# Four of nine weight-sum DMAs issued in the gate phase, and g2 spread over the partitions by two fp32r products

## The chip, the core and the metric

The kernel runs on one core of one Trainium2 chip. A core has a matrix engine (TensorE, PE in the profile), a vector engine (VectorE, DVE), a scalar engine (ScalarE, ACT), a general engine (GpSimd, POOL), an engine that here only issues transfers (SyncE, SP), and 16 DMA engines. SP and POOL both issue DMAs; in the profile SP's are on queue q1 (hardware_dynamic) and POOL's on queue q0 (software_dynamic). The metric is the time of one execution on the device, in microseconds.

## The reference

One layer of a diffusion backbone with a pooling mixer and a SwiGLU channel mixer, all in fp32. x is 1024 tokens by 1024 features, and F = 2816.

```
mod = silu(c) @ mod_w + mod_b            # 1024 x 6144, split in sh1, sc1, g1, sh2, sc2, g2
hx  = x * (1 + sc1) + sh1
ox  = pool_scale * (windowed means of hx, minus hx, per group, @ pool_w)
x   = layer_norm(ALPHA * x + g1 * ox)
h   = x * (1 + sc2) + sh2
gt, up = split(h @ w_in)                 # w_in 1024 x 5632
x   = layer_norm(ALPHA * x + g2 * ((silu(gt) * up) @ w_out))     # w_out 2816 x 1024
```

## The kernel before

**Precision.** Each fp32 operand of a large product is split into an fp32r part (take_hi, a cast on ACT, line 267) and the fp32r rest (take_lo, a subtraction on DVE, line 270). Three fp32r products on PE (high by high, high by low, low by high) then stand for one fp32 product.

**Stages.** From 0 to 92 us of the profile's span the modulation sums, the pooling and the first layer norm of the first 512 tokens are computed. From 92 to 237 the gate phase runs: 11 pairs of 128-wide column blocks of w_in, each with 8 `gate_step`s on PE (line 761), for the first half of the tokens, mixed with the pooling and the layer norm of the second half. From 237 to 551 the first product of the FFN runs in 22 periods, one for each column block of w_in. It is done by a scheme like Strassen's: it takes seven products of 512-wide halves of tokens and features, and sums of blocks, instead of eight products. From 551 to 778 the second product of the FFN (line 1088) runs in seven passes, with the last layer norm.

**Gate phase.** A table of names, `ORDER_OF_ISSUE`, sets the order in which the pieces of this phase are written, and thereby each engine's order. `gate_load` brings 512 KB of w_in (rows of 1 KB) into a tile wi, `gate_hi` and `gate_lo` split it, `gate_step` multiplies. A pair has two loads, one for each half of the features, and two halves of four steps. After the first half, `gate_first` copies the partial sums from PE's banks into the tile pk on ACT (line 766); after the second, `gate_done` applies silu into gk (line 771); `gate_out` writes pk and gk to memory (pd and gd), from where the FFN's periods read them again. ACT takes its casts in the order in which they are written, and so does DVE its subtractions.

**FFN periods.** Period f issues on SP four loads of 256 KB of w_in for period f + 2 (`weights_load`, tile raw), one load of pd or gd, and in periods 5 to 12 a load of mod_w for g2. POOL sums the loaded weights (`all_sums`, four operations); ACT and DVE split the results (w0h, w0l, ws and so on); PE multiplies (`first_product`, line 895). DVE and ACT form the activations in tiles a, whose blocks and sums are stored by SP (a11d, a2d, s21d, s43d), and the stored tiles free the places of the next ones. Big tiles share 45 places, taken in order.

**Weight sums.** The second product needs four sums of blocks of w_out, e1 to e4, each 1408 by 512 (2816 KB). They are built in memory by nine DMAs, `e_step(0)` to `e_step(8)`, issued from POOL (line 1039). Steps 0 and 1 write a block plainly, steps 2, 3, 6, 7 and 8 add a block to what is there (`accum_op`), steps 4 and 5 copy one sum to another. In the kernel before, step n is issued in period 1 + 2n (`E_AT`, `E_EVERY`), behind that period's `all_sums` on POOL. A step that writes the same sum as an earlier one waits for it: 2 for 0, 3 for 1, 4 for 2, 5 for 3, and so on.

**g2.** The modulation row g2 is summed over features as 128 partial rows in the tile acc (`mod_add`, line 491, in periods 6 to 13). In periods 14 and 15 `g2_half` adds the 128 rows and spreads the sum over all partitions: a product of a matrix of ones with acc, in fp32 on PE (line 870), once for each 512 columns. DVE copies each result to g2.

Of the kernel before, what the change touches and what calls it, by code (L numbers as in the profile page):

```python
# [13 lines left out]
F32R = mybir.dt.float32r  # L14
ACT = mybir.ActivationFunctionType
ALU = mybir.AluOpType

P = 128
# [3 lines left out]
KT = D // P  # L22
# [50 lines left out]
gate_step.9 mod_load.34 gate_step.10 mod_load.35 gate_step.11 gate_load.6 gate_load.7 mod_add.29 gate_step.12  # L73
gate_done.0 gate_out.2 gate_step.13 mod_add.30 gate_step.14 mod_add.31 gate_step.15 load_pool_w.2 load_pool_w.3
mod_add.32 gate_hi.6 gate_step.16 mod_load.37 gate_lo.6 gate_first.2 gate_step.17 mod_load.38 gate_out.3 gate_hi.7
gate_step.18 mod_load.39 gate_lo.7 gate_step.19 gate_load.8 gate_load.9 gate_step.20 gate_done.1 gate_out.4
gate_step.21 gate_step.22 mod_add.33 gate_step.23 mod_add.34 gate_first.3 gate_step.24 gate_out.5 gate_step.25
mod_add.35 gate_step.26 gate_hi.8 gate_step.27 gate_load.10 gate_load.11 gate_lo.8 pool_outer.11 gate_done.2
gate_step.28 gate_out.6 gate_hi.9 gate_step.29 gate_lo.9 gate_step.30 gate_step.31 gate_hi.10 gate_lo.10 gate_first.4
gate_step.32 gate_out.7 gate_hi.11 gate_step.33 gate_lo.11 gate_step.34 gate_step.35 gate_load.12 gate_load.13  # L80
gate_step.36 gate_done.3 gate_out.8 gate_step.37 gate_hi.12 gate_step.38 gate_lo.12 gate_hi.13 gate_step.39
gate_first.5 gate_lo.13 gate_step.40 gate_out.9 gate_step.41 gate_step.42 gate_step.43 gate_load.14 gate_load.15
gate_step.44 gate_done.4 gate_out.10 gate_hi.14 gate_step.45 gate_lo.14 gate_step.46 gate_hi.15 gate_step.47
weights_load.0 gate_lo.15 gate_first.6 gate_step.48 gate_out.11 gate_step.49 gate_step.50 gate_step.51 gate_load.16
gate_load.17 all_sums.0 gate_step.52 gate_done.5 gate_out.12 mod_col.3 one_hi.0 one_lo.0 gate_hi.16 gate_step.53
mod_col_done.1 shift_through.0 two_hi.0 pool_inner.56 gate_lo.16 pool_inner.48 gate_hi.17 pool_inner.39 pool_outer.9
pool_inner.57 pool_inner.49 pool_inner.59 gate_lo.17 pool_outer.14 pool_inner.51 pool_outer.12 gate_step.54
shift_through.1 pool_inner.46 pool_inner.38 pool_inner.58 pool_hi.11 pool_inner.50 gate_step.55 two_lo.0 pool_hi.9
gate_first.7 pool_lo.11 gate_step.56 pool_lo.9 gate_out.13 pool_hi.14 pool_inner.60 pool_lo.14 pool_inner.52
pool_hi.12 pool_inner.61 pool_lo.12 pool_inner.53 pool_inner.63 pool_outer.15 pool_inner.55 pool_outer.13  # L90
pool_inner.62 pool_inner.54 pool_hi.15 shift_bank.0 pool_lo.15 pool_hi.13 shift_bank.1 pool_lo.13 gate_step.57
shift_row.0 shift_row.1 gate_step.58 pooled.12 pooled.14 residual.12 bend.0 gate_step.59 gate_load.18 gate_load.19
gate_hi.18 gate_hi.19 residual.14 bend.2 pooled.13 gate_done.6 gate_lo.18 gate_out.14 pooled.15 residual.13 bend.1
pooled.8 residual.15 pooled.10 bend.3 residual.8 gate_step.60 residual.10 gate_lo.19 pooled.9 mean.6 pooled.11
residual.9 spread.6 mean.7 mean.4 gate_step.61 residual.11 spread.7 factor.6 mean.5 gate_step.62 factor.7 spread.4
gate_step.63 p1_load.0 weights_load.1 factor.4 gate_first.8 gate_step.64 gate_out.15 spread.5 gate_step.65 factor.5
norm.6 gate_step.66 keep_row.6 norm.7 gate_step.67 gate_load.20 gate_load.21 norm.4 keep_row.7 norm.5 gate_step.68
keep_row.4 keep_row.5 gate_done.7 gate_step.69 gate_out.16 gate_step.70 gate_hi.20 gate_step.71 gate_lo.20
gate_first.9 gate_step.72 gate_out.17 gate_hi.21 gate_step.73 gate_lo.21 gate_step.74 turned.8 turned.10 scaled_h.8
gate_step.75 scaled_h.10 gate_done.8 turned.12 turned.14 gate_out.18 scaled_h.12 turned.9 scaled_h.14 turned.11  # L100
turned.13 scaled_h.9 turned.15 scaled_h.11 difference.0 gate_step.76 scaled_h.13 scaled_h.15 difference.4 gate_step.77
hidden_hi.4 difference.1 gate_step.78 hidden_hi.5 difference.5 t_hi.0 gate_step.79 gate_first.10 t_lo.0 gate_step.80
gate_out.19 t_hi.4 hidden_lo.4 gate_step.81 difference.2 t_hi.1 gate_step.82 t_hi.5 difference.3 t_hi.2 gate_step.83
t_lo.4 gate_done.9 gate_step.84 t_lo.1 gate_out.20 t_hi.3 gate_step.85 t_lo.5 t_lo.2 gate_step.86 t_lo.3 gate_step.87
gate_done.10 hidden_lo.5 gate_out.21 difference.6 difference.7 t_hi.6 t_lo.6 t_hi.7 t_lo.7
""".split()

ENGINE_OF = {}
# [111 lines left out]
def trunk_kernel(ctx: ExitStack, tc: tile.TileContext, x, c, mod_w, mod_b, ln_g, ln_b, ffn_w_in, ffn_w_out,  # L220
                 pool_w, pool_scale, consts, out):
    nc = tc.nc
    keep = ctx.enter_context(tc.tile_pool(name="keep", bufs=1))
# [34 lines left out]
    def small(name, shape, bufs=1, tag=None):  # L258
        return keep.tile(list(shape), F32, tag=tag or name, name=name, bufs=bufs)
# [12 lines left out]
    def split(hi, lo, src):  # L272
        take_hi(hi, src)
        take_lo(lo, src, hi)
# [16 lines left out]
    tiles = {}  # L291
# [228 lines left out]
    def column_half(h):  # L520
        return slice(h * HALF, (h + 1) * HALF)
# [213 lines left out]
    e_of = [dram.tile([P, NF // 2, HALF], F32, tag=f"e{n}", name=f"ed{n}", bufs=1) for n in range(1, 5)]  # L735
    p1_of, gate_of = spill("p"), spill("g")

    def act_tile(name):
        return take("big", name, F32, (P, 2, HALF))

# [121 lines left out]
    for j in range(2):  # L862
        for n in (1, 3, 2, 4):
            job(difference, n, j)
            job(t_hi, n, j)
            job(t_lo, n, j)

    def g2_half(h):
        ps = bank(f"ps_g2_{h}")
        nc.tensor.matmul(ps, ones, tiles["acc", G2][:, column_half(h)], start=True, stop=True)  # L870
        nc.vector.tensor_copy(g2[:, column_half(h)], ps)
        done_with("bank", f"ps_g2_{h}")

# [148 lines left out]

    first, second = column_half(0), column_half(1)
    whole = slice(0, D)
    w_out = ffn_w_out.rearrange("(j r p) d -> p r j d", p=P, r=2)
    res, lines, raw, operands = {}, {}, {}, {}

    def block(r, h):

        return w_out[:, r, :, column_half(h)]  # L1030


    E_STEPS = [(0, block(0, 1), False), (2, block(0, 1), False), (0, block(0, 0), True), (2, block(1, 1), True),
               (1, 0, False), (3, 2, False), (3, block(0, 0), True), (1, block(1, 1), True), (3, block(1, 0), True)]

    def e_step(n):
        dst, src, add = E_STEPS[n]
        src = e_of[src] if isinstance(src, int) else src
        nc.gpsimd.dma_start(e_of[dst], src, **({"accum_op": ALU.add} if add else {}))


    PARTS = ((lambda j: a11_of[j][:, 0], lambda j: w_out[:, 0, j, first]),
# [133 lines left out]

    E_AT, E_EVERY = 1, 2

    def other_loads(f):
        if f + 2 < NF:
# [62 lines left out]
    with tc.manual_schedule():  # L1245
# [8 lines left out]
        f = NF  # L1254
# [112 lines left out]
```

## Time and profile before

| what | value |
|---|---|
| time, median of 3 runs | 779.75 us (776.33 to 781.9) |
| time of the profiled execution | 779.76 us |
| its span | 778.0 us |
| mean granted clock of PE | 0.954 |
| PE busy | 732.1 us, 94% of the span |
| DVE busy | 571.5 us, 73% |
| ACT busy | 270.5 us, 35% |
| POOL busy | 166.5 us, 21% |
| queue q1 (SP) | 164.97 MB, 61.8% of the 16 engines' span |
| queue q0 (POOL) | 25.95 MB, 15.0% |

Busy times are shares of the span on that engine. PE's clock is what the throttle granted; 1.00 is full speed, and at 0.50 a product takes twice as long. The share of a DMA queue is the time its packets took, divided by that of 16 engines; a share a little over 1 means that all of them are full. Issue rows of SP and POOL begin when the engine issues the transfer; the data move later.

### The profile page before, as it was taken

To read this page: it belongs to the slowest core of one execution; us is meant where nothing else is said; L and a number is where in the kernel's file an instruction comes from. 1 tells how busy PE (TensorE), PEld (TensorE's weight loads), DVE (VectorE), ACT (ScalarE), POOL (GpSimd) and SP (SyncE) were. 2 spreads that over 40 slices of the span, in tenths; PEclk is the share of its full clock that TensorE was granted. 3 is DMA by queue.
4 is the path that set the end of the run, shared out by engine and by line. 5 is a ranking of instruction groups with operands and counts; after the bars stand their busy time and mean duration, and the time that the engine had idled before them with its cause. 6 is when DMAs were issued, how large, how long until landed. Compare 5 with 4: busy or idle time off the path is not lost.

```text
span 778.0 us, 9216 instructions
## 1 busy us (share of the span) xinstructions
PE 732.1 (94%) x3391; PEld 609.7 (78%) x3391; DVE 571.5 (73%) x684; ACT 270.5 (35%) x342; POOL 166.5 (21%) x114
## 2 busy tenths in 40 slices
PE   6939999999999999999999999989999999999991
PEld 6729788888888888887887788768888888888881
DVE  3687734346268888896999796866879659659997
ACT  0324844442983221221221221221557333334201
POOL 0000000020202937164366164260000000000015
PEclk7559999999999999999999999989999999999996
DMA  8999278644636979999999999966899767564202
GB/s 299 351 400 330 109 262 306 230 149 141 228 128 211 339 246 255 288 251 315 330 337 285 262 223 298 208 202 253 284 391 388 274 217 244 187 218 163 109 27 108
DMA packets 117091, 191.51 MB, mean 246 GB/s; under 512 B 7371, under 2 KB 66451, under 8 KB 116918
## 3 DMA queue, kind: packets, MB, share of 16 engines
q1 hardware_dynamic: 108326, 164.97, 61.8%
q0 software_dynamic: 8720, 25.95, 15.0%
q8 instruction: 26, 0.43, 0.2%
q14 instruction: 19, 0.16, 0.1%
HBM read 150.79 MB, written 66.06 MB: 279 GB/s over the span
## 4 chain that ended last, share of the span: by engine, by line
PE 60%; DVE 25%; DMA 7%; issue 3%; ACT 2%; SPq 1%; POOL 0%; POOLq 0%; DVEq 0%; ACTq 0%
PE ps_v L895 17%; PE ps_gate L761 16%; PE ps_x L1088 15%; DMA a11d<-a 4%; PE ps_y L1088 4%; DVE w1l L270 3%; DVE w0l L270 3%; DVE acc L491 2%; DVE ws L270 2%; PE ps_pt L461 2%; DVE ylo L270 2%; DVE yrow L1148 1%; PE ps_ox L263 1%; DVE su L1127 1%; PE ps_ox L264 1%
## 5 line engine op out<-in xcount | busy, mean ns | idle before, releaser
L958 POOL TENSOR_TENSOR s<-raw,raw 128x512 f32<-128x512 f32 x22 | 35.6, 1616 | 353.3 <-DMA raw<-in_ffn_w_in 323.8
L895 PE MATMUL ps_v<-t,w0h 128*128 128x512 f32 x352 | 111.0, 397 | 0.0
L761 PE MATMUL ps_gate<-h,wih 128*128 128x512 f32 x352 | 109.8, 393 | 0.8 <-ACT h L699 0.8
L267 ACT CAST yhi<-yraw 128x1024 fp32r<-128x1024 f32 x77 | 79.3, 1052 | 84.6 <-PE ps_x L1088 32.2
L270 DVE TENSOR_TENSOR ylo<-yraw,yhi 128x1024 fp32r<-128x1024 f32 x77 | 91.5, 1219 | 13.3 <-ACT yhi L267 7.3
L1088 PE MATMUL ps_x<-ylo,yhi 128*128 128x512 f32 (+1 forms) x231 | 87.6, 379 | 0.0
L1088 PE MATMUL ps_x<-yhi 128*128 128x512 f32 (+1 forms) x231 | 87.6, 379 | 0.0
L1088 PE MATMUL ps_x<-yhi,ylo 128*128 128x512 f32 (+1 forms) x231 | 87.5, 379 | 0.0
L918 ACT ACTIVATE a<-a 128x512 f32<-128x512 f32 x22 | 13.9, 632 | 187.7 <-DVE a L917 178.1
L895 PEld LDWEIGHTS ps_v<-t,w0h 128*128 128x128 f32 x352 | 67.2, 191 | 15.0 <-issue 1.0
L761 PEld LDWEIGHTS ps_gate<-h,wih 128*128 128x128 f32 x352 | 65.2, 188 | 14.5 <-ACT h L699 1.0
L491 DVE SCALAR_TENSOR_TENSOR acc<-mw,s_col,acc 128x1024 f32<-128x1024 f32 x40 | 55.3, 1384 | 23.1 <-DMA mw<-in_mod_w 22.9
L895 PE MATMUL ps_v<-t,ws 128*128 128x512 f32 x264 | 66.9, 401 | 4.8 <-DVE ws L270 4.7
L895 PE MATMUL ps_v<-t,w0l 128*128 128x512 f32 x176 | 69.2, 393 | 0.5 <-DVE w0l L270 0.5
L761 PE MATMUL ps_gate<-h,wil 128*128 128x512 f32 x176 | 68.6, 390 | 0.0
L895 PEld LDWEIGHTS ps_v<-t,ws 128*128 128x128 f32 x264 | 50.5, 193 | 17.3 <-DVE ws L270 6.9
L1110 POOL TENSOR_TENSOR yrow<-yrow,line_lg 128x512 f32<-128x512 f32 (+2 forms) x4 | 5.8, 1462 | 239.6 <-ACT yrow L1144 239.6
L895 PE MATMUL ps_v<-h,w1h 128*128 128x512 f32 x176 | 54.2, 389 | 0.0
L895 PE MATMUL ps_v<-t,w1h 128*128 128x512 f32 x176 | 54.2, 389 | 0.0
L1088 PEld LDWEIGHTS ps_x<-ylo,yhi 128*128 128x128 f32 x231 | 43.4, 188 | 8.3
L1088 PEld LDWEIGHTS ps_x<-yhi 128*128 128x128 f32 x231 | 43.4, 188 | 8.2
L1088 PEld LDWEIGHTS ps_x<-yhi,ylo 128*128 128x128 f32 x231 | 43.4, 188 | 8.1
(151 smaller groups left out, 1392.7 us busy)
## 6 DMA issues: line engine op xcount, KB each, us to landing
mw<-in_mod_w SPq DMA_DIRECT2D x48, 512.0 KB, 9.2
raw<-in_ffn_w_in SPq DMA_DIRECT2D x88, 256.0 KB, 7.1
ed<-in_ffn_w_out POOLq DMA_DIRECT2D x7, 2816.0 KB, 22.1
wi<-in_ffn_w_in SPq DMA_DIRECT2D x22, 512.0 KB, 6.8
yraw<-ed SPq DMA_DIRECT2D x44, 256.0 KB, 4.4
yraw<-in_ffn_w_out SPq DMA_DIRECT2D x33, 256.0 KB, 5.5
pd<-pk SPq DMA_DIRECT2D x11, 512.0 KB, 4.9
gd<-gk SPq DMA_DIRECT2D x11, 512.0 KB, 3.1
```

Of the source, the lines that this page charges most:

```text
L263: nc.tensor.matmul(ps, lh, rl, start=False, stop=False)
L264: nc.tensor.matmul(ps, ll, rh, start=False, stop=last)
L267: nc.scalar.copy(hi, src)
L270: nc.vector.tensor_tensor(lo, src, hi.bitcast(F32), ALU.subtract)
L461: nc.tensor.matmul(pt_bank[half, ct][:, a:b], xr[ORDER[half][n]][:, ct * P : (ct + 1) * P], operand, start=n == 0, stop=False, skip_group_ ...
L491: nc.vector.scalar_tensor_tensor(acc, w, s_col[:, k : k + 1], acc, ALU.mult, ALU.add)
L761: nc.tensor.matmul(ps, x, y, start=k == n == 0, stop=k % 4 == 3 and n == 2, skip_group_check=k > 3)
L895: nc.tensor.matmul(ps, x, y, start=fresh and first, stop=last, skip_group_check=not fresh)
L918: nc.scalar.activation(a[:, 1], a[:, 1], ACT.Silu)
L958: nc.gpsimd.tensor_tensor(s, up1, up2, ALU.add)
L1088: nc.tensor.matmul(ps, s[x][:, r * P : (r + 1) * P], t[y][:, d], start=fresh and j == m == 0, stop=j == PAIRS - 1 and m == 2, skip_group_c ...
L1127: nc.vector.bn_stats(st_of[i][:, n, :], res[i][:, s])
```

## The change

Two edits.

1. The first four weight-sum DMAs are issued in the gate phase. A new piece, `e_paced(n, pair)`, stands in the table of the order right behind `gate_first` of pairs 0, 3, 6 and 9. It makes POOL copy one column of that pair's pk tile into a small tile, for which it has to wait until ACT has written pk, and then issues `e_step(n)`. The other five steps are issued in periods 2, 6, 10, 14 and 18 (`E_AT` 2, `E_EVERY` 4). The functions `block` and `e_step` are moved up in the file, without other change.
2. `g2_split` splits acc in period 13, behind its last `mod_add`, by a cast on ACT and a subtraction on DVE. `g2_half` then multiplies the two parts with a matrix of ones in fp32r (`ones_r`, a copy made by ACT at the start).

On POOL, the first rows after the start of the program: before, sums of weights (L958 to L961) stand behind the clearing of acc, and the first weight-sum DMA, ed, follows after three sets of sums.

```order
L382 MEMSET acc_158 128x1024
L958 TENSOR_TENSOR s_1237<-raw_0_1197,raw_1_1200 128x512
L959 TENSOR_TENSOR raw_0_1197<-raw_0_1197 128x512
L960 TENSOR_TENSOR raw_0_1197<-s_1237,raw_0_1197 128x512
L961 TENSOR_TENSOR raw_1_1200<-raw_1_1200,raw_0_1197 128x512
...
L1039 DMA ed_120<-in_ffn_w_out 1408x1x512
L958 TENSOR_TENSOR s_2062<-raw_0_1957,raw_1_1960 128x512
```

In the same place of the changed kernel:

```order
L386 MEMSET acc_161 128x1024
L758 COPY pace<-pk_816 128x1
L754 DMA ed_121<-in_ffn_w_out 1408x1x512
L758 COPY pace<-pk_984 128x1
L754 DMA ed_123<-in_ffn_w_out 1408x1x512
L758 COPY pace<-pk_1212 128x1
L754 DMA ed_121<-in_ffn_w_out 1408x1x512
L990 TENSOR_TENSOR s_1246<-raw_0_1204,raw_1_1207 128x512
...
L758 COPY pace<-pk_1672 128x1
L754 DMA ed_123<-in_ffn_w_out 1408x1x512
```

Three of the early DMAs now stand ahead of the first weight sums, and the fourth behind two sets of them; each has a copy of a pk tile ahead of it, which waits for ACT.

On DVE, at the end of the sums for g2 in period 13, the changed kernel has one more row, the subtraction, between the last sum and the rows that read PE's banks:

```order
L495 SCALAR_TENSOR_TENSOR acc_2376<-mw_7_3118,s_col,acc_2376 128x1024
L272 TENSOR_TENSOR g2l<-acc_2376,g2h 128x1024
L937 TENSOR_TENSOR both_3286<-ps_v_6_3273,p_6_3008 128x512
```

Before, the same place reads:

```order
L491 SCALAR_TENSOR_TENSOR acc_2366<-mw_7_3110,s_col,acc_2366 128x1024
L905 TENSOR_TENSOR both_3275<-ps_v_6_3262,p_6_2999 128x512
L909 TENSOR_TENSOR upb_3277<-ps_v_7_3249,both_3275 128x512
```

The row behind the sum, which frees nothing until it has read a bank of PE, has moved back by one. The diff, with the table of the order cut to two of the four places:

```diff
+E_PACES = (0, 3, 6, 9)
...
-mod_load.32 mod_add.28 gate_first.0 gate_step.7 mod_load.36 gate_out.0 gate_first.1 gate_step.8 mod_load.33 gate_out.1
+mod_load.32 mod_add.28 gate_first.0 e_paced.0 gate_step.7 mod_load.36 gate_out.0 gate_first.1 gate_step.8 mod_load.33
...
-weights_load.0 gate_lo.15 gate_first.6 gate_step.48 gate_out.11 gate_step.49 gate_step.50 gate_step.51 gate_load.16
+gate_step.47 weights_load.0 gate_lo.15 gate_first.6 e_paced.2 gate_step.48 gate_out.11 gate_step.49 gate_step.50
...
     ones = small("ones", (P, P))
+    ones_r = keep.tile([P, P], F32R, tag="ones_r", name="ones_r", bufs=1)
...
     def fill_ones():
         nc.vector.memset(ones, 1.0)
+        nc.scalar.copy(ones_r, ones)
...
+    E_STEPS = [(0, block(0, 1), False), (2, block(0, 1), False), (0, block(0, 0), True), (2, block(1, 1), True),
+               (1, 0, False), (3, 2, False), (3, block(0, 0), True), (1, block(1, 1), True), (3, block(1, 0), True)]
+
+    def e_step(n):
+        dst, src, add = E_STEPS[n]
+        src = e_of[src] if isinstance(src, int) else src
+        nc.gpsimd.dma_start(e_of[dst], src, **({"accum_op": ALU.add} if add else {}))
+
+    def e_paced(n, pair):
+
+        nc.gpsimd.tensor_copy(pace, tiles["pk", pair][:, 0, 0:1])
+        e_step(n)
+
+    pace = small("pace", (P, 1))
...
+    for n, pair in enumerate(E_PACES):
+        job(e_paced, n, pair)
...
+    def g2_split():
+        tiles["g2s",] = [big(f"g2{q}", F32R) for q in "hl"]
+        split(*tiles["g2s",], tiles["acc", G2])
+
     def g2_half(h):
         ps = bank(f"ps_g2_{h}")
-        nc.tensor.matmul(ps, ones, tiles["acc", G2][:, column_half(h)], start=True, stop=True)
+        for n, t in enumerate(tiles["g2s",]):
+            nc.tensor.matmul(ps, ones_r, t[:, column_half(h)], start=n == 0, stop=n == 1)
...
-    E_AT, E_EVERY = 1, 2
+    E_AT, E_EVERY = 2, 4
...
+        if n == KT - 1:
+            g2_split()
         if 0 <= n - KT < 2:
             g2_half(n - KT)
         if n == KT + 2:
-            done_with("big", f"acc{G2}")
+            done_with("big", f"acc{G2}", "g2h", "g2l")
...
-        if (f - E_AT) % E_EVERY == 0 and 0 <= f - E_AT < E_EVERY * len(E_STEPS):
-            e_step((f - E_AT) // E_EVERY)
+        n = len(E_PACES) + (f - E_AT) // E_EVERY
+        if f >= E_AT and (f - E_AT) % E_EVERY == 0 and n < len(E_STEPS):
+            e_step(n)
```

More of the change, by code (lines that the diff above doesn't have):

```diff
@@ L76 @@
[L76 to L80, printed above, removed]
@@ L86 @@
[L86 to L90, printed above, removed]
@@ L91 @@
[L91 to L100, printed above, removed]
@@ new lines @@
+gate_out.1 gate_step.9 mod_load.34 gate_step.10 mod_load.35 gate_step.11 gate_load.6 gate_load.7 mod_add.29
+gate_step.12 gate_done.0 gate_out.2 gate_step.13 mod_add.30 gate_step.14 mod_add.31 gate_step.15 load_pool_w.2
+load_pool_w.3 mod_add.32 gate_hi.6 gate_step.16 mod_load.37 gate_lo.6 gate_first.2 gate_step.17 mod_load.38 gate_out.3
+gate_hi.7 gate_step.18 mod_load.39 gate_lo.7 gate_step.19 gate_load.8 gate_load.9 gate_step.20 gate_done.1 gate_out.4
+gate_step.21 gate_step.22 mod_add.33 gate_step.23 mod_add.34 gate_first.3 e_paced.1 gate_step.24 gate_out.5
@@ new lines @@
+gate_step.25 mod_add.35 gate_step.26 gate_hi.8 gate_step.27 gate_load.10 gate_load.11 gate_lo.8 pool_outer.11
+gate_done.2 gate_step.28 gate_out.6 gate_hi.9 gate_step.29 gate_lo.9 gate_step.30 gate_step.31 gate_hi.10 gate_lo.10
+gate_first.4 gate_step.32 gate_out.7 gate_hi.11 gate_step.33 gate_lo.11 gate_step.34 gate_step.35 gate_load.12
+gate_load.13 gate_step.36 gate_done.3 gate_out.8 gate_step.37 gate_hi.12 gate_step.38 gate_lo.12 gate_hi.13
+gate_step.39 gate_first.5 gate_lo.13 gate_step.40 gate_out.9 gate_step.41 gate_step.42 gate_step.43 gate_load.14
@@ new lines @@
+gate_load.15 gate_step.44 gate_done.4 gate_out.10 gate_hi.14 gate_step.45 gate_lo.14 gate_step.46 gate_hi.15
+gate_step.47 weights_load.0 gate_lo.15 gate_first.6 e_paced.2 gate_step.48 gate_out.11 gate_step.49 gate_step.50
+gate_step.51 gate_load.16 gate_load.17 all_sums.0 gate_step.52 gate_done.5 gate_out.12 mod_col.3 one_hi.0 one_lo.0
+gate_hi.16 gate_step.53 mod_col_done.1 shift_through.0 two_hi.0 pool_inner.56 gate_lo.16 pool_inner.48 gate_hi.17
+pool_inner.39 pool_outer.9 pool_inner.57 pool_inner.49 pool_inner.59 gate_lo.17 pool_outer.14 pool_inner.51
@@ new lines @@
+pool_outer.12 gate_step.54 shift_through.1 pool_inner.46 pool_inner.38 pool_inner.58 pool_hi.11 pool_inner.50
+gate_step.55 two_lo.0 pool_hi.9 gate_first.7 pool_lo.11 gate_step.56 pool_lo.9 gate_out.13 pool_hi.14 pool_inner.60
+pool_lo.14 pool_inner.52 pool_hi.12 pool_inner.61 pool_lo.12 pool_inner.53 pool_inner.63 pool_outer.15 pool_inner.55
+pool_outer.13 pool_inner.62 pool_inner.54 pool_hi.15 shift_bank.0 pool_lo.15 pool_hi.13 shift_bank.1 pool_lo.13
+gate_step.57 shift_row.0 shift_row.1 gate_step.58 pooled.12 pooled.14 residual.12 bend.0 gate_step.59 gate_load.18
@@ new lines @@
+gate_load.19 gate_hi.18 gate_hi.19 residual.14 bend.2 pooled.13 gate_done.6 gate_lo.18 gate_out.14 pooled.15
+residual.13 bend.1 pooled.8 residual.15 pooled.10 bend.3 residual.8 gate_step.60 residual.10 gate_lo.19 pooled.9
+mean.6 pooled.11 residual.9 spread.6 mean.7 mean.4 gate_step.61 residual.11 spread.7 factor.6 mean.5 gate_step.62
+factor.7 spread.4 gate_step.63 p1_load.0 weights_load.1 factor.4 gate_first.8 gate_step.64 gate_out.15 spread.5
+gate_step.65 factor.5 norm.6 gate_step.66 keep_row.6 norm.7 gate_step.67 gate_load.20 gate_load.21 norm.4 keep_row.7
@@ new lines @@
+norm.5 gate_step.68 keep_row.4 keep_row.5 gate_done.7 gate_step.69 gate_out.16 gate_step.70 gate_hi.20 gate_step.71
+gate_lo.20 gate_first.9 e_paced.3 gate_step.72 gate_out.17 gate_hi.21 gate_step.73 gate_lo.21 gate_step.74 turned.8
+turned.10 scaled_h.8 gate_step.75 scaled_h.10 gate_done.8 turned.12 turned.14 gate_out.18 scaled_h.12 turned.9
+scaled_h.14 turned.11 turned.13 scaled_h.9 turned.15 scaled_h.11 difference.0 gate_step.76 scaled_h.13 scaled_h.15
+difference.4 gate_step.77 hidden_hi.4 difference.1 gate_step.78 hidden_hi.5 difference.5 t_hi.0 gate_step.79
@@ L106 @@
+gate_first.10 t_lo.0 gate_step.80 gate_out.19 t_hi.4 hidden_lo.4 gate_step.81 difference.2 t_hi.1 gate_step.82 t_hi.5
+difference.3 t_hi.2 gate_step.83 t_lo.4 gate_done.9 gate_step.84 t_lo.1 gate_out.20 t_hi.3 gate_step.85 t_lo.5 t_lo.2
+gate_step.86 t_lo.3 gate_step.87 gate_done.10 hidden_lo.5 gate_out.21 difference.6 difference.7 t_hi.6 t_lo.6 t_hi.7
+t_lo.7
 """.split()
```

24 lines of the change are left out of this document (3 added, 21 removed).

## The prediction

> **What bounds the kernel now.** I read the page first, then the busy time by stage, then the idle rows of the stage that showed any, then the DMA queues there. The page says that TensorE (PE) is busy nearly all of the time, and its last chain runs through PE, with some VectorE (DVE) and one store:
>
> ```profile
> span 778.0 us, 9216 instructions
> PE 60%; DVE 25%; DMA 7%; issue 3%; ACT 2%; SPq 1%; POOL 0%; POOLq 0%; DVEq 0%; ACTq 0%
> ```
>
> The profiled run took 779.8 us, 1.8 more than its span, and equals the median of the runs shown (779.75), so the sum is made against 779.8 without correction. An edit gains only where PE is idle or slowly clocked, and costs wherever PE starts to wait. The table by stage (window, its length, then busy us of PE, PEld, DVE, ACT and POOL, clock, DMA share, GB/s) separates the two:
>
> ```profile
> 92.00:237.00 145.00, 145.00 (x724) 122.15 (x724) 70.38 (x104) 75.76 (x108) 10.81 (x8) 1.00 0.57 196
> 297.00:437.00 140.00, 136.68 (x591) 111.38 (x590) 124.65 (x125) 31.18 (x40) 71.02 (x44) 0.99 1.03 288
> 437.00:520.00 83.00, 79.12 (x338) 64.02 (x337) 61.98 (x67) 15.92 (x20) 38.69 (x25) 0.97 1.01 256
> ```
>
> In the gate phase (92 to 237) PE never waits, and the DMA engines have room on average, 0.57. In the first FFN product (the two lower rows) the DMA engines are full, over 1.0, and PE is idle 3.32 + 3.88 = 7.2 us. Two of these waits are followed by a halved clock (the rows with a start time are the timeline, with the idle time before and its releaser; the others have the columns of the stage table):
>
> ```profile
> 428.78 1.21 PE L870 MATMUL ps_g<-acc,ones 128*128 128x512 f32 x2 [1.88 <-DVE acc L491]
> 516.27 4.63 PE L895 MATMUL ps_v<-t,ws 128*128 128x512 f32 x10 [3.26 <-DVE ws L270]
> 430.00:433.00 3.00, 3.00 (x8) 2.32 (x8) 2.27 (x5) 1.59 (x3) 0.00 (x0) 0.50 1.13 208
> 515.00:521.50 6.50, 5.23 (x12) 4.13 (x13) 6.02 (x6) 0.38 (x1) 6.26 (x5) 0.50 0.23 95
> ```
>
> At half clock, 3.00 and 5.23 busy us hold half as much work: 1.5 + 2.6 = 4.1 us lost. Together 7.2 + 4.1 = 11.3 us is all that there is to gain from waits in this stage.
>
> Their cause is the nine weight-sum DMAs. Seven read the weights, two copy:
>
> ```profile
> ed<-in_ffn_w_out POOLq DMA_DIRECT2D x7, 2816.0 KB, 22.1
> 301.08 1.74 POOL L1039 DMA_DIRECT2D ed<-in_ffn_w_out  x1
> 452.52 1.71 POOL L1039 DMA_DIRECT2D ed<-in_ffn_w_out  x1
> 484.05 1.71 POOL L1039 DMA_DIRECT2D ed<-in_ffn_w_out  x1
> q0 software_dynamic: 1424, 2.88, 90.1%
> ```
>
> The last row is queue q0 from 304 to 323: the one accumulating step issued at 301.08 takes 90.1% of all engines for 19 us, 17.1 us of all sixteen. While two queues have work, they move packet for packet. These are two stretches, 467 to 469 and 469 to 472, of the step issued at 452.52:
>
> ```profile
> q0 software_dynamic: 99, 0.20, 54.5%
> q1 hardware_dynamic: 96, 0.39, 51.9%
> ...
> q0 software_dynamic: 239, 0.49, 87.6%
> q1 hardware_dynamic: 235, 0.18, 24.7%
> ```
>
> So a load of small packets on q1 proceeds at the pace of the large ones on q0: 239 packets of q0 took 87.6% of 3 us on 16 engines, 0.18 us each. The loads then hold up SyncE (SP), which issues in order, so the store of a11d goes late, and DVE waits for that store and is late with ws for PE:
>
> ```profile
> 494.27 7.99 SPq L880 DMA_DIRECT2D raw<-in_ffn_w_in  x4
> 503.48 2.15 SPq L933 DMA_DIRECT2D a11d<-a  x1
> DVE a L941 <- DMA a11d<-a: 16.9, 3, 7.1
> ```
>
> **Part 1: fewer steps in the FFN stage.** Two plain and two accumulating steps leave it. Three accumulating steps and two copies remain, four periods apart instead of two (before, 452.52 and 484.05 are issues of neighbours, 31.5 us apart). What goes at most is the 11.3 us. What is late next is the same chain, at each accumulating step that is left: five of them cost 11.3 us, or 2.3 each, which would leave 6.8 for three. But the large waits came where the load of one step met the backlog of the one before it; with twice the spacing the backlog has four periods to drain. I leave 1.0 us and count 10.3 as gained, with 4.5 (each step pays its own) and 11.3 as ends.
>
> An issue costs POOL under 2 us (1.74 above). POOL, busy 71.02 of 140, sums weights two periods ahead of their use, so fewer issues there gain nothing, and the small copy that paces each early step is work on an engine with 10.81 busy us of 145 in the gate phase: nothing waits behind it there but the next steps and the first weight sums, which are used after 237. Cost 0 for both; the price, were the sums late, is the issue's 1.7.
>
> **Part 2: g2.** PE's fp32 product per half becomes two fp32r products:
>
> ```profile
> 443.64 1.52 PE L895 MATMUL ps_v<-t,ws 128*128 128x512 f32 x6
> 445.00 1.02 PE L870 MATMUL ps_g<-acc,ones 128*128 128x512 f32 x2
> 445.46 1.03 PE L895 MATMUL ps_v<-t,w0h 128*128 128x512 f32 x2
> 446.33 0.40 PE L895 MATMUL ps_v<-t,w0l 128*128 128x512 f32 x1
> ```
>
> By the starts, six fp32r products take 445.00 - 443.64 = 1.36 us, 0.227 each. From 445.00 to 446.33 lie g2 and two more fp32r products: 1.33 - 0.45 = 0.88 us for g2. Two fp32r products take 0.45, so a half saves 0.43, both 0.9. The new cast on ACT and subtraction on DVE cost what their like do:
>
> ```profile
> L267 ACT CAST yhi<-yraw 128x1024 fp32r<-128x1024 f32 x77 | 79.3, 1052 | 84.6 <-PE ps_x L1088 32.2
> L270 DVE TENSOR_TENSOR ylo<-yraw,yhi 128x1024 fp32r<-128x1024 f32 x77 | 91.5, 1219 | 13.3 <-ACT yhi L267 7.3
> ```
>
> Both lie in the period before g2 is used. ACT is idle most of the stage (31.18 busy of 140). DVE, at 124.65 of 140, is not: behind the subtraction stand the sums that free PE's banks. If DVE is late there as it was at 428.78 (1.88 us), the 1.2 us falls on PE; I take 0, because the first of these waits should go with part 1, and keep 1.2 plus 1.05 = 2.3 as the end. The cast of the ones at the start, with one more table load, lies in an idle stretch of ACT of 4.92 us:
>
> ```profile
> 6.94 0.21 ACT L347 ACTIVATE s_col<-cols 128x8 f32<-128x8 f32 x1 [4.92 <-DVE cols L345]
> ```
>
> That costs 0 as long as the two take under 4.92; two casts of 1.05 would fit twice.
>
> **Part 3: four steps in the gate phase.** Step 0 is issued after the first copy of pk for pair 0, around 100.9, and its data follows about 3 us later, as at 301.08. Its size is that of the plain steps, of which one was seen alone:
>
> ```profile
> q0 software_dynamic: 468, 1.92, 98.7%
> 99.88 2.63 ACT L766 COPY pk<-ps_gate 128x512 f32<-128x512 f32 x4 [4.55 <-PE ps_gate L761]
> q1 hardware_dynamic: 6079, 10.96, 102.8%
> 113.20 1.05 ACT L267 CAST wih<-wi 128x1024 fp32r<-128x1024 f32 x1 [5.24 <-DMA wi<-in_ffn_w_in]
> 114.28 1.22 DVE L270 TENSOR_TENSOR wil<-wi,wih 128x1024 fp32r<-128x1024 f32 x1
> 118.50 0.39 PE L761 MATMUL ps_gate<-h,wil 128*128 128x512 f32 x1
> ```
>
> The first row is 258 to 263: 98.7% of 5 us on 16 engines for 468 packets is 0.169 us each; 2816 KB in 4 KB packets are 704, 44 per engine, 7.4 us. The third row is 102 to 132: q1 alone fills the engines, so here no time is free and the 7.4 us go straight onto the load of pair 3 (cast at 113.20 as soon as it had landed, its low part ready at 115.50, first used at 118.50). It had 3.0 us to spare, so PE waits 7.4 - 3.0 = 4.4 us, and by the two halved stretches above (1.5 and 2.6 us) a slow clock adds about 2.0. Ends: 0, if the queue's backlog is loads that nobody needs soon, and 7.4 + 2.6 = 10.
>
> Step 1 (pair 3, about 124) meets loads that have already been put back by PE's own wait, and q1's backlog ends at 132; I take 0, with 2.5 as an end. Step 3 (pair 9) meets only stores; 0, end 2. Step 2 is an accumulating one, at pair 6:
>
> ```profile
> 156.21 1.27 ACT L766 COPY pk<-ps_gate 128x512 f32<-128x512 f32 x2 [2.03 <-PE ps_gate L761]
> 157.94 1.31 SPq L295 DMA_DIRECT2D wi<-in_ffn_w_in  x2
> 163.33 1.05 ACT L267 CAST wih<-wi 128x1024 fp32r<-128x1024 f32 x1
> 171.63 1.08 ACT L471 CAST pt<-ps_pt 128x512 fp32r<-128x512 f32 x2 [3.27 <-PE ps_pt L461]
> 172.25 1.29 DVE L474 TENSOR_TENSOR pt<-ps_pt,pt 128x512 fp32r<-128x512 f32 x2
> 174.86 1.09 PE L461 MATMUL ps_pt<-consts,x 128*128 128x136 f32 x8
> ```
>
> Its data begins near 160, while the two loads of pair 8 (157.94) are under way. They are 1024 packets of 1 KB, 64 per engine, and each waits for one of q0: 64 x 0.18 = 11.5 us later. ACT takes its casts in order: the one of 163.33 stands ahead of the casts of the pooled tile (171.63), and those free the bank that PE fills at 174.86. With 163.33 + 11.5 = 174.8 for the first cast, the second and the pooled ones follow by about 178, and DVE's low parts behind them. I take the 11.5 less the 163.33 to 171.63 gap's own slack (3.27 idle on ACT, and 174.86 - 172.25 - 0.65 = about 2 between the first pooled low part and the bank's next use): 11.5 - 5 = 6.5 us, and 2.0 for the clock; ends 0 and 11.5 + 2.6 = 14.
>
> The clock terms rest on those two rows. The Trainium skill, "TensorE: Matmul & The Clock Gate", Part 1: The HAM clock gate, has the clock halved after at least one idle window of about 3.4 us; by that, a wait of 4.4 us would seldom hold a whole window, and the sum would be about 2 us lower. The trace disagrees: after 1.88 us of waiting the clock was 0.50.
>
> Sum: 779.8 - 10.3 - 0.9 + (4.4 + 2.0) + (6.5 + 2.0) = 783.5 us; I say 783.
>
> **The rivals.** About 1% (7.8 us, so 772.0 and 787.5) is what a measurement can tell from no change.
> - The gate phase takes it (faster): the loads of pairs 3 and 8 land before their use in spite of q0, since the engines average only 0.57 there and the loads are issued a whole pair ahead. For it: PE has no wait at all there today. Against: the 102.8% from 102 to 132 and the packet counts 239 to 235. The gate terms go, 14.9 in all: 783.5 - 14.9 = 768.6. With step 2 alone absorbed it is 775.
> - Each accumulating step pays for itself (slower): one step of 17.1 us slows two periods' loads whatever its spacing, so a11d is late, and three steps leave 6.8 us instead of 1.0. It decides if the wait for a11d persists with one step per four periods. For it: the wait at 516.27 followed the step issued at 484.05, and the one issued at 452.52 should have been over by then (about 3 us of delay and 17 to 19 of transfer). Then 783.5 + 5.8 = 789.3; with the DVE end of g2, 791.6.
> - The move does nothing: PE's waits in the FFN are due to loads and stores on q1 alone (q1 would need the room by itself), and the gate phase has room: 779 to 781. Against: q0 takes 90.1% of a stretch.
>
> **How the numbers follow.** The wash (forecast, 775 to 788) 0.42; faster rival 0.30; slower rival 0.22; nothing 0.06. Faster by over 1% is the second, 0.30. Slower is the third and the upper tail of the first, 0.22 + 0.07 = 0.29. Within 1% is the rest, 0.41. The range runs from the faster rival less a microsecond and a half, 767, to the slower one with its g2 end and a little more of step 0, 793; past these lie the ends where no term or every term goes wrong. The forecast's own range is 775 to 788.
>
> **What would show it.** In the changed profile PE should have idle rows around 118 to 123 (released by DVE wil or ACT wih) and around 175 to 182 (released by the pooled tile's casts or wih), each followed by a clock below 1.0; the FFN windows should show a DMA share well under 1.0 and idle PE of 1 us or less; the a11d wait should nearly vanish. ps_g should show four products of about 0.23 us. No idle PE from 100 to 237 would prove the faster rival; PE waits for ws or a11d after the steps of periods 10, 14 and 18 the slower one. If the loads of pair 3 land at 113 as before, the packet-for-packet step of my argument is wrong in that place.

## The result

The changed kernel takes 806.2 us (median of 4 runs, 799.7 to 812.0) against 780.8 before (4 runs): 1.032 times the time before, with an interval of 1.026 to 1.037. The run of 812.0 counts as a slow one and is not in the ratio; the other three have a median of 804.1 us, so the change costs 23 us. Its profiled execution took 804.1 us, 24.3 more than that of before. The table by stage of the changed kernel (window, length, then busy us of PE, PEld, DVE, ACT and POOL, clock, DMA share, GB/s):

```profile
92.00:237.00 145.00, 137.49 (x678) 113.93 (x677) 61.77 (x95) 68.57 (x99) 18.11 (x16) 0.99 0.84 259
297.00:437.00 140.00, 134.34 (x583) 110.40 (x582) 113.37 (x119) 28.67 (x37) 62.55 (x40) 0.98 0.83 245
437.00:520.00 83.00, 77.52 (x325) 62.89 (x324) 66.60 (x73) 18.24 (x23) 36.98 (x22) 0.96 0.73 187
520.00:551.00 31.00, 24.56 (x96) 19.38 (x95) 16.43 (x18) 4.71 (x6) 12.62 (x8) 0.83 0.80 215
```

In the gate phase PE is now idle for 7.5 us, which was expected. In the first FFN product, where waits were to vanish, PE is idle for 5.7 + 5.5 + 6.4 = 17.6 us instead of 7.2, though the DMA share there has fallen from 1.03 and 1.01 to 0.83 and 0.73. Half of PE's busy time in the stretches with a halved clock comes to another 1.6 us in the gate phase and 8.6 in the FFN (4.5 before, where the prediction's two windows held 4.1 of it). These differences, 9.1 and 14.5 us, less the 0.9 us that the forecast gave to g2's products, make 22.7 of the 24.3 us; about 1.6 are not traced.

PE's waits over half a microsecond, by the timeline, first those of the gate phase and then those of the FFN:

```profile
122.67 1.22 PE L786 MATMUL ps_gate<-h,wih 128*128 128x512 f32 x2 [4.51 <-ACT wih L269]
184.94 1.56 PE L465 MATMUL ps_pt<-consts,x 128*128 128x136 f32 x8 [2.28 <-DVE pt L478]
...
411.65 0.79 PE L927 MATMUL ps_v<-t,ws 128*128 128x512 f32 x1 [4.67 <-DVE ws L272]
444.78 0.50 PE L902 MATMUL ps_g<-g2h,ones_r 128*128 128x512 f32 x1 [1.28 <-ACT g2h L269]
446.04 0.50 PE L902 MATMUL ps_g<-g2l,ones_r 128*128 128x512 f32 x1 [0.76 <-DVE g2l L272]
477.06 1.27 PE L927 MATMUL ps_v<-t,ws 128*128 128x512 f32 x3 [3.43 <-DVE ws L272]
535.15 0.90 PE L927 MATMUL ps_v<-t,ws 128*128 128x512 f32 x2 [2.22 <-ACT ws L269]
540.26 1.22 PE L927 MATMUL ps_v<-t,ws 128*128 128x512 f32 x2 [4.22 <-DVE ws L272]
```

Left out are a wait of 0.52 at 148 and one of 0.99 at 406. The two rows about 445 are for g2. Each of the three accumulating steps that remain in the FFN is followed by a wait for ws. DVE is late with ws because it waits for the store of a11d, as before the change, but for longer. DVE's waits from 240 to 575 in the changed kernel (total, times, longest) say so:

```profile
DVE a L973 <- DMA a11d<-a: 37.0, 4, 13.7
```

Before, that was 23.6 us in five times, 7.1 at the longest. Why is it longer with fewer steps? SyncE's issues around the same step (number 7) show it, first those of the kernel before (step issued at 452.52), then of the changed one, where it is the second accumulating step, with the step's own issue on POOL:

```profile
462.52 0.32 SPq L951 DMA_DIRECT2D s43d<-a  x1
462.94 7.68 SPq L880 DMA_DIRECT2D raw<-in_ffn_w_in  x4
470.67 0.89 SPq L295 DMA_DIRECT2D gate<-gd  x1
471.66 1.96 SPq L933 DMA_DIRECT2D a11d<-a  x1
473.72 3.20 SPq L880 DMA_DIRECT2D raw<-in_ffn_w_in  x4
```

```profile
444.66 1.71 POOL L754 DMA_DIRECT2D ed<-in_ffn_w_out  x1
451.25 0.32 SPq L983 DMA_DIRECT2D s43d<-a  x1
451.67 11.59 SPq L912 DMA_DIRECT2D raw<-in_ffn_w_in  x4
463.36 1.26 SPq L297 DMA_DIRECT2D gate<-gd  x1
464.71 0.38 SPq L965 DMA_DIRECT2D a11d<-a  x1
```

SyncE takes its work in order. At the end of each odd period it has the store of s43d, and it waits for the sums that this store sends out. Everything written behind it, the loads of the next even period and then those of the odd one, goes out in one burst. In the kernel before, the step had been issued 10.4 us before the burst's first load (462.94 - 452.52), in the changed one 7.0 us (451.67 - 444.66). A step needs some 3 us to start (issue at 301.08, data from 304) and 18 to 20 to run (1424 packets from 304 to 323), so more of it now lies on the burst: the four loads took SyncE 11.59 us to issue instead of 7.68, and a11d stands behind them. That these few microseconds are the cause was a reading; the experiments test it.

### The profile page after: what moved, and what is told of

It reads as the page before. It is cut to its first block, busy times and chain, and to the rows that moved or that the text cites. A ratio compares the mean times of both kernels' runs of the same rounds, so it can differ in the third digit from the quotient of the medians.

```text
span 802.3 us, 9226 instructions
## 1 busy us (share of the span) xinstructions
PE 738.2 (92%) x3391; PEld 613.1 (76%) x3391; DVE 568.4 (71%) x685; ACT 272.7 (34%) x345; POOL 170.6 (21%) x118
## 4 chain that ended last, share of the span: by engine, by line
PE 57%; DVE 19%; DMA 14%; SPq 5%; issue 3%; ACT 2%; POOL 0%; POOLq 0%; DVEq 0%; ACTq 0%
PE ps_v L927 22%; PE ps_x L1106 15%; PE ps_gate L786 11%; DMA mw<-in_mod_w 7%; PE ps_y L1106 4%; SPq L912 3%; DMA a11d<-a 3%; DMA raw<-in_ffn_w_in 2%; DVE acc L495 2%; DMA wi<-in_ffn_w_in 2%; DVE w1l L272 2%; DVE ylo L272 1%; DVE w0l L272 1%; SPq L297 1%; DVE ws L272 1%
## 5 line engine op out<-in xcount | busy, mean ns | idle before, releaser
L927 PE MATMUL ps_v<-t,ws 128*128 128x512 f32 x264 | 70.4, 418 | 15.5 <-DVE ws L272 12.3
L927 PEld LDWEIGHTS ps_v<-t,ws 128*128 128x128 f32 x264 | 52.9, 202 | 29.0 <-DVE ws L272 13.8
L272 DVE TENSOR_TENSOR wil<-wi,wih 128x1024 fp32r<-128x1024 f32 x22 | 26.8, 1224 | 37.1 <-ACT wih L269 34.6
L1106 PEld LDWEIGHTS ps_x<-yhi,ylo 128*128 128x128 f32 x231 | 43.4, 188 | 8.2
## 6 DMA issues: line engine op xcount, KB each, us to landing
mw<-in_mod_w SPq DMA_DIRECT2D x48, 512.0 KB, 10.2
wi<-in_ffn_w_in SPq DMA_DIRECT2D x22, 512.0 KB, 10.3
```

The lines of the kernel that those rows point to most:

```text
L272: nc.vector.tensor_tensor(lo, src, hi.bitcast(F32), ALU.subtract)
L927: nc.tensor.matmul(ps, x, y, start=fresh and first, stop=last, skip_group_check=not fresh)
L1106: nc.tensor.matmul(ps, s[x][:, r * P : (r + 1) * P], t[y][:, d], start=fresh and j == m == 0, stop=j == PAIRS - 1 and m == 2, skip_group_c ...
```

## Experiments

Each was run beside the kernel before on the same chip, and ratios are to that. "Idle" is PE's idle time in the first FFN product, "slow" the half of its busy time at a halved clock there.

**The same five steps in odd periods.**

```diff
-    E_AT, E_EVERY = 2, 4
+    E_AT, E_EVERY = 1, 4
```

> The changed kernel with its last five weight-sum DMAs in periods 1, 5, 9, 13 and 17 instead of 2, 6, 10, 14 and 18; nothing else differs. Theory of the phase (a step that starts in an even period lies over that period's loads, behind which the store of a11d is queued, and the next period's sums wait for that store): the wait for a11d shrinks from about 10 to 14 us at each accumulating step to 0 to 7 as before the change, PE's idle time in the FFN falls from 17.6 to at most 7 us, the time to 786 to 793. Theory of the price per step (each accumulating step costs its stall wherever it starts): idle time and time stay within 3 us of the changed kernel, about 806.

789.0 us, ratio 1.013 (1.008 to 1.019): 15 us less than the changed kernel's 804.1, by one digit in the code. Its table by stage, FFN:

```profile
297.00:437.00 140.00, 140.00 (x620) 115.91 (x619) 125.48 (x129) 31.16 (x40) 66.59 (x41) 1.00 0.83 249
437.00:520.00 83.00, 81.18 (x357) 66.63 (x356) 68.22 (x74) 18.87 (x24) 37.23 (x24) 1.00 0.93 233
```

Idle is 1.85 us, slow 0 (the expectation of a later run speaks of 1.4, which the clock of 1.00 above does not bear out). PE's two waits, 1.06 and 0.76 us, are for g2h and g2l: none lies behind a weight-sum step. SyncE around the second accumulating step of this kernel, with the step's issue:

```profile
434.34 1.71 POOL L754 DMA_DIRECT2D ed<-in_ffn_w_out  x1
450.06 0.32 SPq L983 DMA_DIRECT2D s43d<-a  x1
450.47 3.51 SPq L912 DMA_DIRECT2D raw<-in_ffn_w_in  x4
```

The step starts 16.1 us before the burst and most of it has run when the burst comes: the four loads take 3.51 us to issue. So 7.0, 10.4 and 16.1 us of lead go with 11.59, 7.68 and 3.51 us of issue. The other accumulating steps of the kernels here that have s43d ahead of the loads fall in line: a lead of 2 to 7 us goes with 10.6 to 12.6 us of issue, 10 to 12 with 5.7 to 8.1, some 14 with 4.6 to 5.5, 16 to 18 with 2.7 to 4.0. What PE pays for it is another matter: the third step here has a lead of 10.2 us and 8.06 of issue and costs PE nothing, where a like step before (issued at 484.05) was followed by the wait of 3.26. A price per step, the same wherever it starts, is refuted.

**The kernel before, with all nine steps in even periods.**

```diff
-    E_AT, E_EVERY = 1, 2
+    E_AT, E_EVERY = 2, 2
```

> The kernel before, with all nine weight-sum DMAs one period later (periods 2, 4, .. 18 instead of 1, 3, .. 17). Theory of the phase: each of the five accumulating steps now costs what one costs in the changed kernel (17.6 us idle and about 8 us of slow clock for three, so 8 each), PE idle 20 to 30 us in the FFN, time 800 to 820. Theory of the price per step: as before, 780, within 4 us.

827.2 us, ratio 1.061 (1.057 to 1.065): 48 us over before, above the range that was expected. Idle is 43.4 and slow 15.5 us. DVE's wait for a11d goes with it (240 to 590):

```profile
DVE a L941 <- DMA a11d<-a: 83.3, 7, 14.9
```

The seven waits lie behind the five accumulating steps and the two copies; together they cost PE 59 us, over 8 each on average (5.4 to 8.7 of waiting behind an accumulating step, 2.5 and 4.0 behind the copies, which had cost nothing in the changed kernel). None of the early steps, nor the g2 part, is in this kernel, so neither is needed for the loss.

**g2 alone.** The kernel before with `ones_r`, `g2_split` and the two fp32r products, and nothing else of the change.

> The kernel before with the g2 part of the change alone (acc split by ACT and DVE in period 13, fp32r products). By the sum of the prediction 0.9 us less than before, 779 to 780; if the split on DVE is uncovered, up to 2.3 us more.

778.5 us, ratio 1.001 (0.998 to 1.004): no difference. Its profile shows PE waiting 3.0 us for g2h and 0.5 for g2l, where PE waited 1.88 for acc before. The split lies in the open at that place, and by these rows takes back more than the 0.9 us that the products were to save; in the time neither shows.

**a11d on a queue of its own.** The changed kernel with

```diff
-            nc.sync.dma_start(a11_of[j][:, 0], a[:, 0])
+            nc.scalar.dma_start(a11_of[j][:, 0], a[:, 0])
```

> The changed kernel with only the stores of a11d issued from ScalarE, on a queue of their own, so that they don't stand behind the loads on SyncE's queue. If the queue order is the cause: the wait for a11d falls under 4 us each, PE's idle time in the FFN to 2 to 8 us, the time to 786 to 794. If the loads themselves are what comes late (weights, sums), PE waits as long for ws as in the changed kernel, and the time stays within 3 us of 806. A third outcome: ScalarE, which takes its work in order, is held up by the wait for the activation that is stored, and its casts come late: PE waits for casts instead.

802.7 us, ratio 1.030 (1.027 to 1.034): by the time no different from the changed kernel (1.032), as the second outcome has it. The profile says more: the FFN loses 19.1 us (12.6 idle, 6.5 slow) instead of 26.2, but the gate phase, whose program is the same, 17.1 instead of 9.1, and so hides the 7 us gained. DVE's wait for a11d is gone, but another takes its place. PE waits after the first and the third accumulating step:

```profile
413.81 0.73 PE L927 MATMUL ps_v<-t,ws 128*128 128x512 f32 x2 [2.27 <-ACT ws L269]
...
539.82 0.73 PE L927 MATMUL ps_v<-t,ws 128*128 128x512 f32 x2 [3.81 <-ACT ws L269]
```

ACT in turn waited 9.6 us for POOL's sum (413.13, ws), and POOL waited 24.3 us for raw, until 411.84: SyncE needed 11.84 us, from 392.60 on, to issue the four loads. ACT was held up by its own store too (3.7 us ahead of the cast at 394.00), but not where PE waited; there it was the late loads. In a burst under a step both the store behind the loads and the loads are late, and freeing the store alone takes away about a quarter of the FFN's loss in this profile.

**s43d behind the next loads.** The changed kernel, steps in even periods, with one transfer moved in SyncE's order:

```diff
     def period(f):
         other_loads(f)
+        if f % 2 == 0 and f > 3:
+            a_more_out((f - 4) // 2)
...
         if pair is not None:
             a_more_sums(pair)
-            a_more_out(pair)
+            if f == NF - 1:
+                a_more_out(pair)
```

> The changed kernel (steps in even periods) with one transfer moved on SyncE: the store of s43d goes behind the next period's loads instead of ahead of them, so that these loads no longer wait on SyncE for the sums that are stored. If the even period is bad because SyncE, held by that store, sends the loads of two periods in one burst at the even period's start, PE's idle time in the FFN falls from 17.6 us to 8 or less and the time to 788 to 798. If the even period is bad only because its own store of a11d stands behind its own loads, the wait for a11d and the time stay, 802 to 810.

780.9 us, ratio 1.002 (0.999 to 1.005): 23 us less than the changed kernel, more than was expected. In the profiled execution, which at 775.7 us was the fastest of ten, idle is 0.9, slow 0, and DVE waits 8.0 us for a11d instead of 37.0. SyncE still waits at s43d, 55.8 us from 240 to 550 instead of 106.8, but what PE needs first no longer stands behind it. SyncE's issues in this kernel, the gate loads and raw now ahead of s43d:

```profile
455.02 2.70 SPq L912 DMA_DIRECT2D raw<-in_ffn_w_in  x4
457.82 2.36 SPq L297 DMA_DIRECT2D gate<-gd  x1
464.48 0.34 SPq L983 DMA_DIRECT2D s43d<-a  x1
466.17 0.32 SPq L965 DMA_DIRECT2D a11d<-a  x1
```

**The same in the kernel before.** That edit alone, and then with the steps in even periods as well.

> The kernel before with the one transfer moved on SyncE (the store of s43d behind the next period's loads), all nine steps in odd periods as before, nothing of the change. If SyncE's order was what made the loads come in bursts, the FFN's loss of 7.2 us idle and 4.5 us of slow clock falls to 4 or less together and the time to 768 to 773. If the DMA engines are simply full there (a share over 1.0 from 297 to 520 in the kernel before), the time stays at 777 to 783.

771.8 us, ratio 0.990 (0.987 to 0.994); idle 2.5, slow 1.7 us, together 4.2 where at most 4 were expected.

> The kernel before with all nine steps in even periods (827 us, 48 over before) and the store of s43d behind the next period's loads. If the even period is bad only through the burst of loads that SyncE sends once it is past that store, nearly all of the 48 us go, and the time is within 6 us of the kernel with odd periods and the store moved (771.8): 768 to 778. If half or more of them are due to something else in the even period (its own store of a11d behind its own loads, or POOL's sums), 795 or more.

766.8 us, ratio 0.983 (0.977 to 0.989). What cost 48 us costs nothing once the store stands behind the loads: 827.2 with it ahead of them, 766.8 with it behind. DVE's wait for a11d goes from 83.3 us to this (240 to 550), and SyncE's order around step 7, which POOL issues at 456.19, is the one below it:

```profile
DVE a L941 <- DMA a11d<-a: 2.3, 1, 2.3
...
445.65 5.51 SPq L880 DMA_DIRECT2D raw<-in_ffn_w_in  x4
451.22 2.42 SPq L295 DMA_DIRECT2D gate<-gd  x1
455.12 0.34 SPq L951 DMA_DIRECT2D s43d<-a  x1
456.82 0.32 SPq L933 DMA_DIRECT2D a11d<-a  x1
457.25 2.71 SPq L880 DMA_DIRECT2D raw<-in_ffn_w_in  x4
```

The even period's loads now go out ahead of the step, and a11d ahead of the next ones. Loads still meet the steps: under three of the accumulating ones four loads take some 8 to 10 us to issue, SyncE's own waits taken off, and PE does not wait for them. So slow loads alone cost nothing here. The move of the store did two things, loads earlier and a11d earlier, and the runs don't fully separate them; a11d alone was worth 7 of 26 us in the one profile above. The table by stage:

```profile
92.00:237.00 145.00, 145.00 (x723) 122.14 (x723) 71.00 (x104) 75.69 (x108) 10.33 (x8) 1.00 0.57 196
297.00:437.00 140.00, 140.00 (x618) 115.54 (x617) 122.24 (x130) 30.70 (x41) 72.87 (x45) 1.00 1.04 298
437.00:520.00 83.00, 83.00 (x366) 68.36 (x365) 60.66 (x70) 18.84 (x24) 33.69 (x22) 1.00 1.03 262
```

The DMA engines are as full as in the kernel before (1.04 and 1.03), all nine steps are in the FFN, and PE never waits. So the share over 1.0 that the prediction started from was not what bound PE there.

**Which steps cost in the gate phase.** Three kernels with the FFN's steps in odd periods and the early ones behind other pairs; the diff is of the first, the second has (0, 3, 9) and the third (3, 5, 6, 9):

```diff
-E_PACES = (0, 3, 6, 9)
+E_PACES = (3, 5, 9)
...
-    E_AT, E_EVERY = 2, 4
+    E_AT, E_EVERY = 1, 4
```

> The changed kernel with only three early steps, behind the first halves of pairs 3, 5 and 9, and the other six in the odd periods 1, 5, 9, 13, 17 and 21. If the gate phase loses time only where a step meets loads that are needed at once (pairs 0 and 6), PE waits 1 us or less between 92 and 237, the FFN loses 2 to 5 us (1.85 idle and 1.4 of slow clock in the run with odd periods, one accumulating step more here), and the time is 770 to 777, faster than before. If any step in the gate phase costs its 4 to 8 us, 783 or more.

> The same with the early steps behind pairs 0, 3 and 9, so that the first step lies at pair 0 again. By the sum of the prediction it costs 4.4 us of waiting and 2.0 of slow clock: 6 to 9 us over the run with pairs 3, 5 and 9, the wait at about 122.

> Early steps behind pairs 3, 5, 6 and 9, five later ones in the odd periods 1, 5, 9, 13 and 17: the third, accumulating step lies at pair 6 as in the changed kernel, but none at pair 0. By the prediction's sum the step at pair 6 costs 6.5 us of waiting and 2.0 of slow clock; the changed kernel showed 2.3, the run with odd periods 5.8. So 3 to 9 us over the run with pairs 3, 5 and 9; if step 0's and step 2's costs add up, the two differences together give the 789 of the run with odd periods within 3 us.

786.1 us (ratio 1.008, 1.005 to 1.012), 783.3 (1.006, 1.003 to 1.009) and 788.2 (1.010, 1.007 to 1.014). The first missed its expectation by 9 us. Its profile, of the fastest of its nine executions (780.9 us), shows two reasons, and leaves the other 5 us of the median open. A step behind pair 5 isn't free, and a step in period 21 falls on the first loads of the second product:

```profile
168.84 1.54 PE L510 MATMUL ps_col<-ones,acc 128*128 128x64 f32 x6 [3.68 <-ACT gk L796]
...
549.67 0.50 PE L1106 MATMUL ps_x<-ylo,yhi 128*128 128x512 f32 x1 [3.20 <-DVE ylo L272]
```

The second, with the same step in period 21, has a wait of 4.19 us there. The first one's FFN proper (four accumulating steps, odd periods) has no idle time at all; that of the second and third loses 7.2 and 7.6 us, of which a wait for ws of 1.8 and 2.0, waits for g2's split of 3.8 and 2.2, and a slow clock for the rest. The second and the third therefore can't be set against it as was planned; their own profiles price the places. The step at pair 0 costs a wait of 5.46 us (and the clock 2.6), the one at pair 6 a wait of 6.12. Over the five profiled executions with a step at pair 6, the wait for the pooled tile was 1.0, 2.3, 4.7, 5.8 and 6.1 us, so that price varies from one kernel and execution to the next. The step behind pair 3 cost 0.5 to 0.9 us of waiting in four profiles and nothing in four, and the one behind pair 9 nothing.

**The version that follows.** The changed kernel with the two plain steps early, behind pairs 3 and 9, the other seven in periods 1, 4, .. 19, and the store of s43d moved.

> The changed kernel with two early steps only, the two plain ones, behind pairs 3 and 9, seven later ones in periods 1, 4, 7, .. 19, and the store of s43d behind the next period's loads. The step behind pair 3 cost 0.5 us of waiting where it was tried, the one behind pair 9 none; the FFN lost 0.9 us with the store moved. So PE waits 1 us or less in the gate phase and 0 to 4 in the FFN, and the time is 764 to 772, faster than both kernels. If every step in the FFN has its price whatever SyncE's order, seven steps there cost as much as the nine before did: 776 or more.

767.2 us, ratio 0.985 (0.982 to 0.988), faster than both kernels, by 12 and some 37 us. Its gate phase and FFN:

```profile
92.00:237.00 145.00, 144.29 (x718) 120.94 (x717) 71.50 (x104) 74.30 (x106) 13.78 (x12) 1.00 0.69 236
297.00:437.00 140.00, 140.00 (x619) 115.89 (x618) 123.70 (x133) 33.66 (x44) 66.60 (x43) 1.00 0.97 290
437.00:520.00 83.00, 83.00 (x367) 68.68 (x367) 67.74 (x75) 17.86 (x24) 34.62 (x23) 1.00 0.97 258
```

It is no faster than the kernel with nine steps in the FFN and the store moved (766.8): once the loads stand ahead of s43d, taking steps out of the FFN gains nothing that these runs can tell.

## Why the prediction was wrong

The forecast was 783 us, within 1%, with a range to 793; the time was 806.

- **What bounds the kernel: right in the chain, wrong in the cause.** PE's idle time, the late ws, the wait for a11d and SyncE's order were as read. But "the loads then hold up SyncE" was the wrong way round for the start of it: SyncE had been held first, by s43d, and sent its loads in a burst. The view of waits that gave the a11d row has this for SyncE (before, from 240 to 550), and I didn't use it:

```profile
SPq L951 <- DVE a L948: 117.9, 10, 14.5
```

- **Part 1 failed.** The step was: "with twice the spacing the backlog has four periods to drain. I leave 1.0 us and count 10.3 as gained". What mattered most was where in the pair of periods a step starts, and the change had moved that, from odd to even, along with the spacing. I took `E_AT` as a detail. With even periods the FFN's loss rose to 26.2 us, 22.5 of it outside g2's waits and the clock behind them, where 1.0 was left. With odd periods the term came out: the loss fell from 11.7 to 1.9 us, 9.8 gained where 10.3 were forecast. In the three other versions of the change with odd periods (early steps behind pairs 3, 5 and 9; 0, 3 and 9; 3, 5, 6 and 9) it was 0, 7.2 and 7.6 us, g2's split and its clock included. Spacing alone did not help: in even periods a step cost about as much with four periods to the next (22.5 us for three) as with two (59 us for five and two copies).
- **The slower rival was nearer, with the wrong mechanism.** It had 0.22 and 789 us. A price per accumulating step of 2.3 us explains neither 26.2 us for three in even periods nor 1.9, none of it behind a step, for three in odd ones; and its price was read from the odd phase only. The even phase wasn't in the trace of before, so the price should have been given an upper end from what a step can do at worst: cover a burst whole.
- **Part 3, the gate phase: right for step 0, in size and place.** A wait of 4.4 us at about 118 to 123 was forecast, 4.51 at 122.67 came; the cast went from 113.20 to 121.58, 8.4 later, 7.4 forecast. The clock's share was 2.0 in the forecast and 1.6 here. Queue q0 took 44.7% of the 16 engines from 103 to 121, 8.0 us, and this whole time fell on the load, as was forecast. Packet for packet was not needed for that and is not what the counts show here: from 105 to 111 q0 moved 330 packets and q1 157. Step 2 was forecast at 6.5 us: 2.3 in this profile, 1.0 to 6.1 over all; a low price here and a high one there are chance as far as these runs tell. Its 2.0 us of slow clock did not come in this profile. Steps 1 and 3 were put at 0 and cost 0.5 and 0. All of the gate terms together: 14.9 forecast, 9.1 in this profile, 17.9 in that of the kernel with odd periods (10.8 idle, 7.1 slow).
- **Part 2, g2: the cover failed.** The cast and the subtraction weren't hidden: 1.28 + 0.76 = 2.0 us of wait, near the end of the bound (2.3) and not the 0 that I took, though little more than the 1.88 us that PE waited for acc there before. The 0.9 us on the products doesn't show by itself in any run. I had let the cover rest on part 1, which failed; but in the kernel with g2 alone it was in the open too. Of the nine profiles with the split, seven have a wait there, of 0.8 to 3.8 us, and two have none (early steps behind pairs 3, 5 and 9, and the version that follows).
- **The clock terms: right for step 0, not for step 2.** A wait of 1.28 + 0.76 us was followed by this (446.8 to 450.2 of the changed kernel):

```profile
446.80:450.20 3.40, 3.40 (x9) 2.63 (x8) 2.67 (x5) 1.53 (x3) 0.00 (x0) 0.50 0.97 132
```

So 2 us of waiting, in two parts, can be followed by 3.4 us at half clock. It isn't a rule: after the 2.28 us at 184.94 in the same profile, and after 2.47 at 416.45 in the kernel with nine steps in even periods, the clock stayed at 1.00. What decides between them is not shown. Of the Trainium skill ("TensorE: Matmul & The Clock Gate", Part 1: The HAM clock gate), the length of the window, 3.4 us, agrees; that a whole window has to be idle does not.

- **What would show it.** The signs named for the slower rival, waits for ws after the steps of periods 10, 14 and 18, are the ones that came, and the fall of the DMA share came with them: a lower share was no sign of success, since PE waited, and so fetched less, per microsecond.

## What to carry to other kernels

When a transfer is moved, look at when the other queue sends, not only at how much: where an engine that issues in order is held by one store, its loads go out in bursts, and a move by one period can turn a large transfer from the gap into the burst. A DMA share of 1 is no bound by itself: here it was 1.03 with 11.7 us lost and 1.04 with none. First see what the issuing engine waits for, and whether a store that has to wait for its data can be written behind the loads that don't.

## What was not expected of the hardware

Where an accumulating step was issued 2 to 7 us ahead of them, the issue of four loads by SyncE took 10.6 to 12.6 us, against 2.7 to 4.0 where it was issued 16 to 18 us ahead: a busy pair of queues shows itself in the issuing engine, and everything behind it, stores that others wait for included, is late by that much. It costs only where something urgent stands behind: with s43d moved and nine steps in even periods, four loads took some 8 to 10 us under three steps, and PE lost nothing. A step of 17 us of all engines' time can so cost PE over 8 us of waiting (4.49 + 4.18 about 380 to 385 in the kernel with nine steps in even periods), or nothing, by when it starts and by what stands behind the loads. A wait near 2 us was followed by a halved clock in some places (1.28 + 0.76, 2.04 and 2.54 us) and not in others (2.02, 2.28 and 2.47). The wait at pair 6 varied between 1.0 and 5.8 us among four kernels whose programs are alike up to there; what decides it stays open.
